# A layer with expert retrieval on one core: 32 more tokens gathered, 352 instead of 384 through all experts, gates in blocks of 16

## The chip, the core and the metric

The kernel runs on one NeuronCore of a Trainium2 chip. The core has a matrix engine (TensorE, PE in the profile; PEld is its weight load), a vector engine (VectorE, DVE), a scalar engine (ScalarE, ACT), GpSimd (POOL), which here only issues gathers, and SyncE (SP), which issues the other transfers; 16 DMA engines move the data of all queues. Each engine works through its own list of instructions in order and waits on semaphores of the others. The metric is device time in microseconds.

## What is computed

One decoder layer on 512 tokens of width 1024 in float32: a gated short convolution beside differential attention, cross-attention to 256 memory tokens, and a channel mixer that retrieves experts. The change lies in the mixer:

```python
def chunk(hc):                                    # 128 tokens
    q = (hc @ w_pq).reshape(PEER_CHUNK, PEER_HEADS, 2, PEER_DK_HALF)
    sc = jnp.einsum('thcd,chnd->thcn', q, sub_keys).astype(jnp.float32)
    vals, idx = lax.top_k(sc, PEER_TOPK)
    cand = vals[:, :, 0, :, None] + vals[:, :, 1, None, :]
    ...
    g = jax.nn.softmax(top_s, axis=-1)
    ue = peer_u[experts]
    ve = peer_v[experts]
    act = jax.nn.gelu(jnp.einsum('td,thkd->thk', hc, ue).astype(jnp.float32), approximate=False)
    return jnp.einsum('thk,thkd->td', (g * act).astype(ve.dtype), ve)
```

Each token takes 8 heads x 16 = 128 of the 16384 experts; an expert is a row of 1024 of `peer_u` and one of `peer_v`. The layer's sum is normed at the end and multiplied by `final_g`.

## The kernel before

Matrix products run in three passes of float32r: both operands are split into a high part (`hi`, ScalarE, L98) and a rest (`lo`, VectorE, L99).

The mixer treats its tokens in two ways. The first 128 tokens gather their experts' rows: for each of the 128 slots one indirect DMA brings 128 rows, one for each partition (512 KB, L825). A u row is multiplied with the token and reduced to a number on VectorE (L808); 16 of them at a time go through Gelu (L811, L812). A v row is added with its weight to an accumulator (L819). The other 384 tokens (`TY`) meet all experts: for each of 128 columns j of the 128 x 128 grid of experts an up-projection (`stage_u`: 24 matmuls of 384 columns, L120, then Gelu, L702) and a down-projection (18 matmuls of 512 columns, L757), with the activations multiplied by gates in between (L746) that are zero for experts not chosen.

The stages in order of time: selection (`keys_scores`, `keys_pairs`, on VectorE above all, with 40 up-projections beside it on TensorE), gates (`gates`), and the down loop (`experts`).

`gates` builds a 128 x 128 table for each token from one-hot rows, four tokens in a group: squares and a Relu on ScalarE (L857, L858), comparisons on VectorE (L862, L863), four matmuls (L864), a copy from PSUM (L865). Six groups make a block of `TB` = 24 tokens, which is written to DRAM (L866). Up-projections run between the groups, `BY_BLOCK` = 3 for each block.

The down loop goes over j = 0 to 127. Each j loads and splits a table of v (L740, L98, L99), reloads an activation that was spilled (L717; 64 of the 128 were spilled, L705), multiplies, splits, and does 18 matmuls. The 32 up-projections of the last columns run from j = 85 to 116, 11 ahead of their use; four more end before the loop. The gates come back for eight j at a time (L738).

The gathers are a generator, `gathered`, to which the stages `send` a number of rows: 4 for each pair of heads (`X_HEAD`), `X_BLOCK` = 3 for each block of gates, and the rest spread over the j, with weight `XW` = 3 where up-projections run beside. That is 16, 48 and 192 of 256 rows; in the loop one row for each j up to 84 and three for each from 85 to 116. A `send` copies the indices of its rows into a small tile `now` (L805; tag `e`, five buffers shared with the loop's products), works off the rows of the `send` before, and issues its own gathers. A v row's weight is copied into `now` of the `send` that works it off (L815):

```python
w = fl[:, k : k + 1]
nc.vector.tensor_copy(w, wx[:, 1, s - P : s - P + 1])
```

The order of each engine's list is made by a scheduler from this program, so instructions may stand earlier or later than they are written. At the end each block of 128 tokens gets its residual added (L771), is squared and summed (L772), goes through a root in 12 small steps, and is scaled and written (L778, L779).

## Time and profile before

| | |
|---|---|
| three runs | 2082.74, 2091.25, 2091.6 us; median 2091.25 |
| the profiled execution | 2089.85 us, of which the span of its instructions is 2088.1 |
| mean granted TensorE clock | 0.992 |
| busy | PE 96%, PEld 85%, DVE 72%, ACT 48%, POOL 17% |
| selection, with up-projections | about 880 to 1020 us |
| gates | about 1020 to 1352 us |
| down loop, one row for each j | about 1368 to 1738 us; u rows to about 1640, then v rows |
| down loop with up-projections, three rows for each j | about 1738 to 2014 us |
| rest of the loop, and the end | 2014 to 2088 us |

Times in the views are microseconds from the span's start. A matmul's duration overlaps with the next one's, so its price is taken from how many follow each other in a stretch. The idle time ahead of an instruction and what ended it stand in brackets in a timeline.

### The profile page before, as it was taken

The numbers are of one execution on the slowest core, as the hardware profiler recorded it, in microseconds if no ns is written. First come the engines' busy times: TensorE is split into PE (matmuls) and PEld (weight loads), VectorE is DVE, ScalarE is ACT, GpSimd is POOL, SyncE is SP. The second block draws the span as 40 slices with busy tenths as digits, with TensorE's granted clock in tenths as the row PEclk, the third lists the DMA queues.
The fourth block names the chain that finished last, engine by engine and source line by source line (L and its number), as shares of the span: only waits on it lengthen the run. The fifth ranks groups of instructions, "written<-read, shape, count | busy, mean of one in ns | idle before, by whom it ended". The sixth has DMA issues, their size and how long they took to land.

```text
span 2088.1 us, 29190 instructions
## 1 busy us (share of the span) xinstructions
PE 2012.8 (96%) x10341; PEld 1765.4 (85%) x10341; DVE 1503.5 (72%) x3531; ACT 1010.7 (48%) x1732; POOL 354.0 (17%) x309
## 2 busy tenths in 40 slices
PE   8999999999999999999999999999999998998997
PEld 7888888888888788999999889988877777888985
DVE  6666666423455689998787676567887776987897
ACT  6654555322344443433499999933333332332333
POOL 1000000000000000013221110022222333664440
PEclk9999999999999999999999999999999999999998
DMA  8422222334332142356778776599999888999984
GB/s 310 137 86 78 89 86 71 93 99 141 117 97 73 61 136 84 113 200 223 241 264 291 252 269 233 202 341 339 335 350 332 309 270 293 334 339 341 358 289 151
DMA packets 162418, 440.11 MB, mean 211 GB/s; under 512 B 14808, under 2 KB 70120, under 8 KB 160224
## 3 DMA queue, kind: packets, MB, share of 16 engines
q1 hardware_dynamic: 124464, 300.98, 42.9%
q0 software_dynamic: 37808, 137.26, 18.3%
q8 instruction: 81, 1.33, 0.3%
q14 instruction: 65, 0.53, 0.1%
HBM read 394.13 MB, written 46.68 MB: 211 GB/s over the span
## 4 chain that ended last, share of the span: by engine, by line
PE 47%; DMA 15%; DVE 14%; ACT 12%; issue 9%; POOL 3%; SPq 0%; ACTq 0%; DVEq 0%; POOLq 0%
PE psmm L120 33%; DMA raw<-in_peer_v 5%; ACT slot L865 5%; DMA res<-in_peer_v,e 4%; DVE lo L99 3%; PE pslg L120 3%; PE psmm L757 3%; ACT sq L857 3%; ACT hi L98 2%; PE pstr L757 2%; DMA res<-in_peer_u,e 1%; DMA act<-sp 1%; ACT oh L858 1%; DMA oh<-in_peer_v,e 1%; DVE acc L819 1%
## 5 line engine op out<-in xcount | busy, mean ns | idle before, releaser
L98 ACT ACTIVATE hi<-raw 128x1024 fp32r<-128x1024 f32 x388 | 409.8, 1059 | 605.0 <-PE psmm L120 302.1
L99 DVE TENSOR_TENSOR lo<-raw,hi 128x1024 fp32r<-128x1024 f32 x388 | 473.4, 1221 | 264.5 <-ACT hi L98 258.9
L120 PE MATMUL psmm<-A,hi 128*128 128x512 f32 x1408 | 445.9, 393 | 1.9 <-DVE Yb L457 1.9
L120 PE MATMUL psmm<-n,hi 128*128 128x384 f32 x1472 | 394.2, 345 | 1.9 <-ACT sp L702 1.9
L120 PEld LDWEIGHTS psmm<-A,hi 128*128 128x128 f32 x1408 | 262.7, 188 | 54.7 <-DVE Yb L457 2.1
L120 PE MATMUL psmm<-A,lo 128*128 128x512 f32 x704 | 277.9, 395 | 0.0
L120 PEld LDWEIGHTS psmm<-n,hi 128*128 128x128 f32 x1472 | 269.3, 190 | 2.4 <-ACT sp L702 2.3
L120 PE MATMUL psmm<-n,lo 128*128 128x384 f32 x736 | 253.0, 344 | 5.0 <-DVE lo L99 4.8
L825 POOL DMA_INDIRECT res<-in_peer_u,e x85 | 94.7, 1114 | 450.5 <-DVE e L805 422.6
L120 PEld LDWEIGHTS psmm<-A,lo 128*128 128x128 f32 x704 | 132.4, 188 | 25.2
L98 ACT ACTIVATE tr<-e 128x384 fp32r<-128x384 f32 x128 | 66.5, 520 | 179.2 <-DVE e L746 173.7
L757 PE MATMUL psmm<-hi,tr 128*128 128x512 f32 x384 | 128.4, 400 | 21.6 <-ACT hi L98 12.4
L120 PE MATMUL pslg<-n,hi 128*128 128x384 f32 x576 | 148.3, 338 | 0.0
L120 PEld LDWEIGHTS psmm<-n,lo 128*128 128x128 f32 x736 | 139.5, 190 | 7.9 <-DVE lo L99 7.8
L808 DVE CUSTOM_DVE_ANT_0 res<-res,hx 128x1024 f32<-128x1024 f32 x101 | 122.6, 1220 | 23.3 <-DMA res<-in_peer_u,e 15.8
L757 PE MATMUL psmm<-lo,tr 128*128 128x512 f32 x384 | 130.2, 393 | 0.0
L825 POOL DMA_INDIRECT res<-in_peer_v,e x74 | 106.4, 1438 | 117.6 <-DVE e L815 93.0
L825 POOL DMA_INDIRECT res<-in_peer_u,kp x16 | 20.4, 1278 | 611.3 <-DVE kp L805 548.2
L757 PE MATMUL psmm<-hi,e 128*128 128x512 f32 x384 | 119.3, 396 | 1.6 <-DVE e L805 1.6
L120 PEld LDWEIGHTS pslg<-n,hi 128*128 128x128 f32 x576 | 105.3, 188 | 3.1
L863 DVE TENSOR_SCALAR oh<-iota,e 128x128 f32<-128x128 f32 x384 | 107.1, 347 | 0.0
L757 PEld LDWEIGHTS psmm<-hi,tr 128*128 128x128 f32 x384 | 71.3, 190 | 40.0 <-ACT hi L98 13.9
(301 smaller groups left out, 3759.4 us busy)
## 6 DMA issues: line engine op xcount, KB each, us to landing
raw<-in_uT SPq DMA_DIRECT2D x128, 512.0 KB, 4.4
raw<-in_peer_v SPq DMA_DIRECT2D x128, 512.0 KB, 5.3
raw<-in_w_in SPq DMA_DIRECT2D x64, 512.0 KB, 3.5
gates<-slot SPq DMA_DIRECT2D x16, 1536.0 KB, 6.8
slot<-gates SPq DMA_DIRECT2D x16, 1536.0 KB, 11.9
act<-sp SPq DMA_DIRECT2D x64, 192.0 KB, 3.8
raw<-in_w_pq SPq DMA_DIRECT2D x16, 512.0 KB, 3.5
raw<-in_w_ckv SPq DMA_DIRECT2D x12, 512.0 KB, 7.7
```

Source lines behind the costliest of these rows:

```text
L98: self.nc.scalar.activation(hi, src, AF.Copy)
L99: self.nc.vector.tensor_tensor(out=lo, in0=src, in1=hi.bitcast(F32), op=ALU.subtract)
L120: self.nc.tensor.matmul(out, ww[:, k, :], xx, start=(k == 0 and p == 0), stop=(k == KC - 1 and p == 2))
L757: nc.tensor.matmul(accs[2 * i + half], l[:, ts], m[:, half * 512 : half * 512 + 512], start=(jj == 0 and p == 0), stop=(jj == NK - 1 and p ...
L808: nc.vector.tensor_tensor_reduce(out=t, in0=t, in1=hx, op0=ALU.mult, op1=ALU.add, scale=1.0, scalar=0.0, accum_out=wx[:, 0, s : s + 1])
L819: nc.vector.scalar_tensor_tensor(out=acc, in0=t, scalar=w, in1=acc, op0=ALU.mult, op1=ALU.add)
L825: nc.gpsimd.indirect_dma_start(out=t, out_offset=None, in_=a["peer_u"] if s < P else a["peer_v"], in_offset=bass.IndirectOffsetOnAxis(ap=i ...
L857: nc.scalar.activation(sq[:, w, :], self.iota, AF.Square, bias=it[:, t0 + w : t0 + w + 1], scale=-1.0)
L858: nc.scalar.activation(oh[:, 0:NA, :], sq, AF.Relu, bias=1.0, scale=-1.0)
L863: nc.vector.tensor_scalar(out=oh[:, 4 + w, :], in0=self.iota, scalar1=cols[:, 0, t - b * TB : t - b * TB + 1], scalar2=cols[:, 1, t - b * ...
L865: nc.scalar.copy(stage[:, :, q * 4 : q * 4 + 4].rearrange("p j w -> p w j"), pp.rearrange("p (w j) -> p w j", w=4))
```

## The change

160 tokens gather instead of 128, and 352 meet all experts instead of 384 (`MORE` = 32). The 32 additional tokens are a second set: their 128 slots lie in quarters on the partitions (partition 32 q + t holds slots 32 q to 32 q + 31 of token t), so one gather brings four rows for each of 32 tokens, and 32 gathers of u and 32 of v do them; a matmul with `quads` (four 32 x 32 identities above each other) adds the quarters at the end. Rows are now a list of jobs: 128 u, 128 v, 32 u, 32 v, 320 in all. `X_BLOCK` is 5 and there are 22 blocks of 16 tokens, so 16 + 110 rows come before the loop and 194 in it. Where there were four row buffers there are five from the gates stage on (`rx`), seven in the loop as before. Up-projections have 352 columns; `BY_BLOCK` is 2.2, and 22 blocks take 48 of them as 16 blocks of three did. The down-projection keeps 18 matmuls of 512 columns, a third of them for 96 tokens. The gates lie in DRAM in blocks of 16, so that the pieces read back are 8 x 16 instead of 8 x 24 numbers. At the end there are five parts instead of four.

```diff
-TY = NY * P
+MORE = 32
+TY = NY * P - MORE
-BY_BLOCK = 3
+BY_BLOCK = 2.2
-X_BLOCK = 3
+X_BLOCK = 5
-TB = 24
+TB = 16
...
+    def second_set(self):
+
+        nc = self.nc
+        xi, xj, xg = (e[0:MORE, 0].rearrange("p h k -> p (h k)") for e in self.e)
+        self.ex1, self.xg1 = self.t("ex1", [P, 32], I32), self.t("xg1", [P, 32])
+        for q in range(4):
+            ps, qs = slice(32 * q, 32 * q + 32), slice(32 * q, 32 * q + 32)
+            nc.vector.scalar_tensor_tensor(out=self.ex1[ps], in0=xi[:, qs], scalar=float(NK), in1=xj[:, qs], op0=ALU.mult, op1=ALU.add)
+            nc.vector.tensor_copy(self.xg1[ps], xg[:, qs])
...
-        left = 2 * P - self.rows_done
+        left = self.rows_all - self.rows_done
...
-                    ts = slice(i * P, (i + 1) * P)
+                    ts = slice(max(i * P - MORE, 0), (i + 1) * P - MORE)
+                    n = ts.stop - ts.start
...
+        quads = self.t("oh", [P, P])
+        nc.sync.dma_start(out=quads, in_=a["quads"])
+        more = [self.ps("lg") for _ in range(2)]
+        for half in range(2):
+            nc.tensor.matmul(more[half][:MORE], quads[:, :MORE], self.acc1[:, half * 512 : half * 512 + 512], start=True, stop=True)
+
+        parts = [(0, slice(0, P), [self.accx[:, :512], self.accx[:, 512:]]), (1, slice(0, MORE), more), (1, slice(MORE, P), accs[0:2])]
+        parts += [(i, slice(0, P), accs[2 * i - 2 : 2 * i]) for i in range(2, NT)]
...
+        jobs = [(0, k, v) for v in (False, True) for k in range(P)] + [(1, k, v) for v in (False, True) for k in range(32)]
+        self.rows_all = len(jobs)
...
+            if sets[1] is None and upto > 2 * P:
+                self.acc1 = self.t("acc1", [P, D])
+
+                hx1 = self.t("hx", [P, D])
+                for q in range(4):
+                    nc.sync.dma_start(out=hx1[32 * q : 32 * q + 32], in_=self.hx1)
+                sets[1] = (32, self.ex1, hx1, self.xg1, self.t("wx1", [P, 2, 32]), self.acc1)
...
-        self.turn = "e"
+        self.turn, self.tags = "e", ("rx",)
...
-        self.tags = ("oh", "oh", "row")
+        self.tags = ("oh", "oh")
```

How the lists change is shown at three places; line numbers are those of each kernel. First VectorE in the gates stage, a stretch of one block before: `oh` are one-hot rows, `res` gathered rows that are reduced against `hx`, `lo` the split of an up-projection's weights.

```order
L862 TENSOR_SCALAR oh_9706<-iota,tr_9349 128x128
L863 TENSOR_SCALAR oh_9706<-iota,e_9701 128x128 x4
L99 TENSOR_TENSOR lo_9882<-raw_9879,hi_9881 128x1024
L808 ISA res_7708,wx_7709<-res_7708,hx_6529 128x1024
L808 ISA wx_7709 128x1
L850 COPY e_10361<-tr_9355 128x24
L850 COPY e_10361<-tr_9361 128x24
L862 TENSOR_SCALAR oh_9723<-iota,tr_9349 128x128
L863 TENSOR_SCALAR oh_9723<-iota,e_9701 128x128 x4
```

And after, of the same stage:

```order
L910 TENSOR_SCALAR oh_9646<-iota,tr_9369 128x128
L911 TENSOR_SCALAR oh_9646<-iota,e_9624 128x128 x4
L856 ISA res_7719,wx_7720<-res_7719,hx_6529 128x1024
L856 ISA wx_7720 128x1
L856 ISA rx_9455,wx_7720<-rx_9455,hx_6529 128x1024
L856 ISA wx_7720 128x1
L100 TENSOR_TENSOR lo_9856<-raw_9853,hi_9855 128x1024
L851 COPY e_10112<-ex_7721 128x5
L856 ISA res_7719,wx_7720<-res_7719,hx_6529 128x1024
L856 ISA wx_7720 128x1
L910 TENSOR_SCALAR oh_9663<-iota,tr_9369 128x128
```

More than one reduction now stands between two groups of one-hot rows, and a gather takes five index columns at once; the last reduction of the stage stands ahead of its last six groups.

Second, VectorE in the down loop, a j of the first 85; before, with u rows (`slot` holds gates, `ex` the indices):

```order
L746 TENSOR_TENSOR e_13468<-B_8070,slot_13460 128x384
L99 TENSOR_TENSOR lo_13465<-raw_13462,hi_13464 128x1024
L808 ISA res_7708,wx_7709<-res_7708,hx_6529 128x1024
L808 ISA wx_7709 128x1
L99 TENSOR_TENSOR e_13471<-e_13468,tr_13470 128x384
L805 COPY e_13492<-ex_7710 128x1
```

After, three j later in the loop:

```order
L851 COPY e_13627<-ex_7721 128x1
L863 COPY e_13627<-wx_7720 128x1
L764 TENSOR_TENSOR e_13638<-B_8247,slot_13525 128x352
L100 TENSOR_TENSOR lo_13635<-raw_13632,hi_13634 128x1024
L867 SCALAR_TENSOR_TENSOR acc_13307<-res_7719,e_13627,acc_13307 128x1024
L100 TENSOR_TENSOR e_13641<-e_13638,tr_13640 128x352
L851 COPY e_13662<-ex_7721 128x1
L863 COPY e_13662<-wx_7720 128x1
L764 TENSOR_TENSOR e_13673<-B_8280,slot_13525 128x352
L867 SCALAR_TENSOR_TENSOR acc_13307<-rx_9455,e_13662,acc_13307 128x1024
```

The reduction of a u row has become the addition of a v row, which takes its weight from the index tile of the j in which it stands; the row itself was gathered with the index tile before. In the list of before the same pattern begins with the v rows, at about j = 64.

Third, TensorE at the end of the program; before:

```order
L757 MATMUL pspv_13176<-lo_18969,tr_18974 128x512
L757 MATMUL pstr_13175<-hi_18968,e_18975 128x512
L757 MATMUL pspv_13176<-hi_18968,e_18975 128x512
L940 UNCONDITIONAL_BRANCH
```

And after:

```order
L776 MATMUL pspv_13233<-lo_19068,tr_19073 128x512
L776 MATMUL pstr_13232<-hi_19067,e_19074 128x512
L776 MATMUL pspv_13233<-hi_19067,e_19074 128x512
L789 MATMUL pslg_19118<-acc_3195_17473,oh_19116 32x512
L789 MATMUL pslg_19119<-acc_3195_17473,oh_19116 32x512
L989 UNCONDITIONAL_BRANCH
```

The two matmuls with `quads` stand behind the last accumulation; on VectorE the additions of their results stand behind those of the last block, and the small steps of four parts follow in turns.

## Rows read from the trace of the kernel before

**Rows 1.** The page, busy time by engine and the DMA share in 40 slices
```profile
PE 2012.8 (96%) x10341; PEld 1765.4 (85%) x10341; DVE 1503.5 (72%) x3531; ACT 1010.7 (48%) x1732; POOL 354.0 (17%) x309
...
DMA  8422222334332142356778776599999888999984
```

**Rows 2.** Busy time by stage: stretch, its length, busy us (instructions), clock, DMA
```profile
core 0: us, PE busy (x) PEld busy (x) DVE busy (x) ACT busy (x) POOL busy (x), PEclk, DMA share, GB/s
880.00:1020.00 140.00, 134.05 (x740) 131.42 (x739) 125.90 (x342) 48.58 (x68) 25.23 (x19) 0.99 0.62 202
1020.00:1352.00 332.00, 316.92 (x2000) 306.62 (x1999) 236.69 (x671) 315.14 (x588) 48.96 (x45) 0.99 0.72 254
...
1400.00:1640.00 240.00, 235.34 (x1023) 191.27 (x1021) 190.64 (x338) 86.15 (x115) 61.59 (x56) 1.00 0.96 338
1640.00:1738.00 98.00, 91.93 (x392) 72.70 (x391) 74.54 (x131) 33.20 (x45) 33.52 (x22) 1.00 0.84 286
1700.00:1738.00 38.00, 34.43 (x147) 26.92 (x146) 28.20 (x49) 12.54 (x17) 12.56 (x9) 1.00 0.81 270
1738.00:2014.00 276.00, 263.18 (x1292) 235.76 (x1292) 228.12 (x353) 91.52 (x126) 148.57 (x98) 0.98 0.91 330
...
2075.00:2088.00 13.00, 0.00 (x0) 0.00 (x0) 9.54 (x49) 3.23 (x12) 0.00 (x0) 0.58 0.35 132
```

**Rows 3.** Chain that ended last: start, us, what; matmuls of 256, 512, 384 columns
```profile
55.65 3.77 PE psmm L120 x32
...
399.60 219.48 PE psmm L120 x961
...
1978.31 4.24 PE pslg L120 x24
```

**Rows 4.** Timelines of VectorE and of ScalarE in the gates stage: start, us, engine, line, operation
```profile
1040.08 1.22 DVE L808 CUSTOM_DVE_ANT_0 res<-res,hx 128x1024 f32<-128x1024 f32 x1
...
1041.39 0.28 DVE L862 TENSOR_SCALAR oh<-iota,tr 128x128 f32<-128x128 f32 x1
1041.59 1.11 DVE L863 TENSOR_SCALAR oh<-iota,e 128x128 f32<-128x128 f32 x4
1042.61 1.22 DVE L808 CUSTOM_DVE_ANT_0 res<-res,hx 128x1024 f32<-128x1024 f32 x1
...
1041.08 1.42 ACT L865 COPY slot<-pstr 128x512 f32<-128x512 f32 x1
1042.21 0.61 ACT L858 ACTIVATE oh<-sq 128x384 f32<-128x384 f32 x1
1042.71 0.98 ACT L857 ACTIVATE sq<-iota,tr 128x128 f32<-128x128 f32 x3
1043.58 1.05 ACT L98 ACTIVATE hi<-raw 128x1024 fp32r<-128x1024 f32 x1
```

**Rows 5.** DMA of 1020 to 1352 us, then of 1372 to 1500, there in 40 slices too
```profile
DMA packets 23353, 84.32 MB, mean 254 GB/s; under 512 B 2592, under 2 KB 9120, under 8 KB 21404
...
GB/s 403 409 393 399 252 384 300 298 294 353 350 393 401 390 288 277 234 341 322 251 306 373 366 403 404 373 307 367 374 302 264 336 365 397 405 345 265 315 285 355
DMA packets 19921, 43.64 MB, mean 341 GB/s; under 512 B 1575, under 2 KB 12071, under 8 KB 19912
```

**Rows 6.** VectorE's waits, 1400 to 1640 us, then 1640 to 1738: total, times, longest
```profile
DVE res L808 <- DMA res<-in_peer_u,e: 5.5, 5, 1.7
...
DVE acc L819 <- DMA res<-in_peer_v,e: 5.4, 3, 2.5
```

**Rows 7.** VectorE's timeline, 2030 to 2068 us: first and last multiplication of eight
```profile
2031.11 0.55 DVE L746 TENSOR_TENSOR e<-A,slot 128x384 f32<-128x384 f32 x1
...
2065.25 0.56 DVE L746 TENSOR_TENSOR e<-A,slot 128x384 f32<-128x384 f32 x1 [1.30 <-DMA res<-in_peer_v,e]
```

**Rows 8.** Timeline of the end: the last accumulation, the last scaling of two halves
```profile
2074.37 0.40 PE L757 MATMUL pspv<-hi,e 128*128 128x512 f32 x1
...
2083.40 1.42 DVE L778 SCALAR_TENSOR_TENSOR hi<-B,misc,hx 128x512 f32<-128x512 f32 x2
```

More of the change, by code (lines that the diff above doesn't have):

```diff
@@ L152, in inverse_root @@
         st = self.t("rt", [P, 8])
+        st = st[: out.shape[0]]
         v, w = st[:, 0:n], st[:, 4 : 4 + n]
@@ L673, in by_token @@
         self.x3 = self.dram.tile([NT, P, D], F32, name="x3")
-        self.hx = self.t("hx", [P, D])
+        self.hx, self.hx1 = self.t("hx", [P, D]), self.dram.tile([MORE, D], F32, name="hx1")
         for i in range(NT):
@@ L795, in gathered @@
             upto = done + more
-            if len(rows) == 4 and "row" in self.tags:
-                rows += [self.t(tag, [P, D]) for tag in self.tags]
-            assert more <= len(rows)
+            rows += [self.t(tag, [P, D]) for tag in self.tags]
+            self.tags = ()
+            if done <= P < upto:
+                self.accx = self.t("acc", [P, D])
+                sets[0] = (*sets[0][:5], self.accx)
+            if sets[1] is None and upto > 2 * P:
[4 more added lines that the diff above has]
+                sets[1] = (32, self.ex1, hx1, self.xg1, self.t("wx1", [P, 2, 32]), self.acc1)
@@ L800, in gathered @@
+            assert more <= min(len(rows), 8)
             now = self.t(self.turn, [P, 16], I32)
             fl = now[:, 8:16].bitcast(F32)
-            for s in range(done, upto):
-                if s == done or s == P:
-                    m = min(upto, P if s < P else upto) - s
-                    nc.vector.tensor_copy(now[:, s - done : s - done + m], ex[:, s % P : s % P + m])
-            for k, (s, t) in enumerate(pend):
-                if s < P:
-                    nc.vector.tensor_tensor_reduce(out=t, in0=t, in1=hx, op0=ALU.mult, op1=ALU.add, scale=1.0, scalar=0.0, accum_out=wx[:, 0, s : s + 1])
-                    if s % 16 == 15:
-                        sl = slice(s - 15, s + 1)
+            k = done
@@ new lines, in gathered @@
+            while k < upto:
+                z, c, v = jobs[k]
+                m = 1
+                while k + m < upto and jobs[k + m][0] == z and jobs[k + m][2] == v:
+                    m += 1
+                nc.vector.tensor_copy(now[:, k - done : k - done + m], sets[z][1][:, c : c + m])
+                k += m
+            for k, ((z, c, v), t) in enumerate(pend):
+                n, _, hx, g, wx, acc = sets[z]
+                if not v:
+                    nc.vector.tensor_tensor_reduce(out=t, in0=t, in1=hx, op0=ALU.mult, op1=ALU.add, scale=1.0, scalar=0.0, accum_out=wx[:, 0, c : c + 1])
+                    if c % 16 == 15:
+                        sl = slice(c - 15, c + 1)
@@ L817, in gathered @@
+                    if c == 0:
                         nc.vector.tensor_scalar(out=acc, in0=t, scalar1=w, scalar2=None, op0=ALU.mult)
@@ L927, in layout @@
     z["buckets"] = _buckets()
+    z["quads"] = np.ascontiguousarray(np.tile(np.eye(32, dtype=f), (4, 4)))
     return z
```

57 lines of the change are left out of this document (32 added, 25 removed), and 2 rows, old and new, of the table TAGS.

## The prediction

> **What bounds the kernel now.** I read the page's busy shares and its slices first, then the busy table by stage, then the chain of waits for the price of a matmul, then the waits and the order of VectorE inside the two stages that the change touches. TensorE is busy 96% of the span [rows 1], but that says little, because its matmuls are pipelined; what counts is how many end per microsecond. The chain gives the price of one behind another: 0.228 us for 512 columns, 0.177 for 384, 0.118 for 256 [rows 3]. So 384 to 352 columns saves 32 x (0.1767 - 0.1178) / 128 = 0.0147 us, 0.162 each.
>
> Four stretches matter [rows 2]. From 880 to 1020 us (selection of the pairs) VectorE is busy 125.9 of 140 us while TensorE runs up-projections beside it: both are near full. From 1020 to 1352 (gates) ScalarE is busy 315.1 of 332: it is the bound there, with VectorE at 236.7 and DMA at 0.72. From 1400 to 1738 (down-projection, one gathered row for each j) the period is set by TensorE and DMA together while u rows arrive: 1023 matmuls at 18 for a j in 240 us are 4.22 us a j against 18 x 0.228 = 4.11, with DMA at 0.96. As soon as v rows arrive the same loop takes 392 matmuls in 98 us, 4.50 us a j, with DMA down to 0.84: nothing is full, something waits. From 1738 to 2014 (down- and up-projection, three v rows for each j) it is 276 / 32 = 8.6 us a j against 18 x 0.228 + 24 x 0.177 = 8.35.
>
> **The wait in the v rows.** VectorE runs in order. A u row is only reduced, and the reduction stands some two j later in the order; a v row must be added with a weight that lies in the small index tile of the next j, so the addition stands right behind the next index copy (both orders are shown ahead). If the row hasn't landed, all of VectorE stands, and with it the split of the next gated activations that TensorE needs. The waits show it: additions wait 5.4 us for rows in res alone in the 98 us of v rows, reductions 5.5 us in the 240 us of u rows [rows 6]. In the last stretch, where DMA is at 0.6 or so, VectorE's own beat from multiplication to multiplication is (2065.25 - 2031.11) / 7 = 4.88 us, eight rows being seen [rows 7]; from 1700 to 1738, where most additions stand one index copy behind their gather, 147 matmuls in 38 us are 4.65 us a j [rows 2].
>
> **The change, part by part.** The sum is made against the profiled execution, 2089.85 us (span 2088.1), 1.4 us below the median of the three runs, 2091.25.
>
> (1) Up to the gates. TensorE saves 24 x 0.0147 = 0.353 us for each up-projection, 14.1 us for the 40 that run here. VectorE gives only part of it back: it is idle 14.1 us of 140 [rows 2], and the change adds to it two multiplications of 512 columns, 0.61 each as half of one of 1024, and eight small ones at 0.28: 3.5 us [rows 4]. VectorE's chain of selections is then what ends last; I take -1, between -6 (half of its idle time goes) and +3.
>
> (2) Gates. A group of four tokens costs ScalarE 2.50 us (copy, Relu, three squares: 1041.08 to 1043.58) and VectorE 1.22 us (1041.39 to 1042.61) [rows 4]. Eight groups of 96 go: -20 us of ScalarE, -10 of VectorE. 62 more u rows are gathered and reduced here (126 instead of 64 before the down loop): at 1.15 us each, 1040.08 to 1041.23, that is +71 us of VectorE. Three or four up-projections run earlier, -5 on each. So ScalarE comes to about 290, VectorE to 236.7 + 71 - 10 - 5 + 2 = 295. DMA: a gather is 128 rows of 4 KB, 0.524 MB; 84.3 + 62 x 0.524 - 2.1 (gates) - 0.9 (spilled activations) - 2.7 (fewer weights) = 111 MB. The highest rate that a long stretch holds is 338 to 341 GB/s [rows 2, 5], so 111 MB want 326 to 329 us: DMA becomes the bound of this stage, at almost the length that ScalarE gives it now. The last blocks' gathers are ordered ahead of the last groups, so DMA runs below its rate at the end; I add 8: 336 against 332, +4. Bounds: VectorE's 295 at the 0.95 that ScalarE reaches now, 310, is -22; 348 (DMA at 319) is +16. The hidden gain of 20 us of ScalarE is thus spent. Sixteen-token blocks make more and shorter writes, of the same rate by the packets; no cost. The gates come back in 512-byte pieces instead of 768, 22 x 128 packets for 16 x 128; at most 37% on a transfer of some 4.6 us of DMA each 8 j, 0.2 us a j, and inside the next term's bounds.
> The Trainium skill ("DMA: Bandwidth & Descriptors", section Where 436 GB/s comes from) puts the limit between HBM and SBUF at about 358 GB/s. By that the 111 MB would want 310 us, and the sum would be 2121 - 18 = 2103, inside the forecast's own range; the longest full stretch here holds 341, so the rows don't reach the page's figure.
>
> (3) Down loop, the 85 j with one row. As many rows as before, but 84 of them are v rows of the first 128 tokens, where 62 of the 85 were u rows. Now: 62 x 4.22 + 23 x 4.50 = 365 us. After: in the new order every addition stands one index copy behind its gather, so I take a beat between the 4.65 of that pattern and the 4.88 of VectorE alone, nearer the first, since about half of the additions have a weight split between: 4.70 x 85 = 399.5, +34. Bounds: 4.22 (the wait is hidden) gives -6; 5.0, 4.88 and the reloads of activations that share DMA, as they don't in either stretch, +60. The load of the second set's h, four 128 KB transfers on SP's queue, waits for the last u reduction; behind it in that queue stand the weights of j 4, which need a split behind the same reduction anyway: no cost.
>
> (4) The 32 j with up-projections: 32 x 0.353 = 11.3 us if TensorE alone decides, and 4 x 0.353 for the four at the start. DMA is at 0.91 and 330 GB/s [rows 2]; at 341 the stretch would be 267, -9. I take -9 in all, between -11 and 0.
>
> (5) Tail. Four chains of small steps instead of three end together, since the 32 tokens' sums are ready last: two multiplications by quads behind the last accumulation and about 17 more VectorE instructions behind it, at 9.54 / 49 = 0.19 us [rows 2], partly pipelined: +3, between +1 and +6. The last accumulation starts at 2074.37 and the last scaling at 2083.40 [rows 8]; all of that is on the path.
>
> Sum: -1 + 4 + 34 - 9 + 3 = +31; 2089.85 + 31 = **2121 us**.
>
> **Rivals.**
> A. The v rows hide as the u rows do: term 3 is -6, and the whole is 2089.85 - 1 + 4 - 6 - 9 + 3 = 2081. For it: the waits by name [rows 6] explain only part of 0.28 us a j, and some of it may be the change from u to v. Against it: the beat of 4.88 with DMA little loaded [rows 7].
> B. The gates stage goes at VectorE's pace and A holds too: 2081 - 26 = 2055, **faster**. It decides from the point where DMA moves over 365 GB/s for 300 us; single slices do, no long stretch does. If the gates stage does so and term 3 stands, 2095, no change. The skill's figure named above lies between this and my bound.
> C. Worse: the beat of the v rows is 5.0, since the reloads lengthen the landing, and the gates stage takes 348: 2121 + 12 + 26 = 2159.
> D. The change doesn't do what it says: a matmul of 352 columns costs what one of 384 does, because the weight load beside it decides. Term 4 goes, term 1 is +3: 2121 + 13 = 2134. Against it: 256 columns run at 0.118 with the same loads [rows 3].
>
> **How the numbers follow.** Forecast, with D in its range (2100 to 2145): 0.52. A: 0.17. B: 0.10, and its half with term 3 standing 0.05. C: 0.16. A run of this kernel tells 0.5% (10.5 us) from no change; below 2080.8 is faster, above 2101.7 slower. A splits evenly over that lower line, so faster 0.10 + 0.08 = 0.18; same 0.09 + 0.05 + 0.02 of the forecast's lower end = 0.16; slower 0.66. The range 2074 to 2160 leaves out B and the far end of C, about 0.18.
>
> **What would show it.** Matmuls of 352 columns 0.162 us apart (D if 0.177). In the gates stage DMA at 0.95 or more and ScalarE idle by over 30 us (B if ScalarE or VectorE is full). In the first 85 j a period of 4.6 to 4.9 us, DMA at 0.8 to 0.9, and VectorE's additions waiting for gathered rows; A if it is 4.2 with DMA at 0.96. After the last accumulation 16 us instead of 13.3. The forecast is wrong if that loop doesn't slow down.

## The result

The changed kernel takes 2169.9 us, median of four runs (2163.5 to 2173.1), against 2089.9 of the kernel before (median of four): a ratio of 1.039, 95% interval 1.036 to 1.042. The profiled execution took 2172.17 us, with a span of 2170.4. So it is slower by 80 us where 31 were forecast, outside the range.

The page of the changed kernel, rows as in [rows 1]: busy time by engine, then granted clock and DMA share in 40 slices of 54 us.

```profile
PE 2005.9 (92%) x10281; PEld 1726.4 (80%) x10281; DVE 1564.8 (72%) x3667; ACT 958.4 (44%) x1698; POOL 434.3 (20%) x373
...
PEclk9999999999999999998887999999999999999998
DMA  8422222343321343567998877798899978999974
```

TensorE lost four points of busy share. The gates stage lies in slices 19 to 26: the clock is lower in slices 19 to 22, and DMA stands at 0.9 in slices 20 and 21 and at 0.7 to 0.8 behind them, up to slice 26. The first matmul or the first transposition of each stage, read from both timelines, splits the 82.3 us of span:

| stretch | before | after | difference | forecast |
|---|---|---|---|---|
| start to the first transposition of the gates stage | 1020.3 | 1019.7 | -0.6 | -1 |
| to the first down-projection matmul | 348.2 | 404.4 | **+56.2** | **+4** |
| to the first up-projection inside the down loop (85 j) | 369.8 | 397.5 | +27.7 | +34 |
| to the last accumulation | 336.1 | 331.4 | -4.7 | -9 |
| tail | 13.7 | 17.4 | +3.7 | +3 |

Four of five terms are near; the gates stage is not. Its row, and those of the two parts of the down loop, answer to [rows 2]: stretch, its length, busy us (instructions), granted clock, DMA share, GB/s.

```profile
core 0: us, PE busy (x) PEld busy (x) DVE busy (x) ACT busy (x) POOL busy (x), PEclk, DMA share, GB/s
1020.00:1404.00 384.00, 308.02 (x1857) 296.50 (x1856) 299.06 (x778) 263.21 (x544) 134.45 (x105) 0.89 0.82 290
1424.00:1820.00 396.00, 370.40 (x1572) 279.88 (x1573) 287.58 (x506) 127.05 (x173) 104.83 (x84) 0.99 0.87 296
1822.00:2153.00 331.00, 310.65 (x1541) 267.00 (x1540) 269.44 (x441) 110.70 (x158) 145.75 (x107) 0.97 0.87 311
```

Over the whole gates stage nothing is full any more: ScalarE 263 of 384 us (it was 315 of 332), VectorE 299, DMA 0.82 of its time at 290 GB/s, TensorE's granted clock 0.89 where it had been 0.99. A stage that is longer than the busy time of each of its engines is a chain of waits. ScalarE's longest waits of that stretch, then VectorE's (what waited, on whom: us in total, times, longest):

```profile
ACT hi L99 <- PE psmm L121: 50.1, 21, 4.8
ACT slot L913 <- PE psmm L912: 21.4, 10, 5.9
...
ACT sp L720 <- DMA act<-sp: 13.1, 8, 4.7
...
DVE res L856 <- DMA res<-in_peer_u,e: 35.8, 21, 6.2
```

The last two have their like in the kernel before, 1020 to 1352 us:

```profile
ACT sp L702 <- DMA act<-sp: 8.6, 8, 2.7
...
DVE res L808 <- DMA res<-in_peer_u,e: 6.7, 5, 2.2
```

Two kinds of transfers are waited for: gathered rows (VectorE), and the spill of an up-projection's result to HBM (ScalarE, which can't write sp again before the last spill has landed). One block shows both, in timelines of POOL, SyncE's queue, ScalarE, VectorE and TensorE around 1200 to 1215 us (start, duration, engine and line; in brackets the idle time before it and what ended it):

```profile
1199.93 1.67 POOL L873 DMA_INDIRECT res<-in_peer_u,e  x1 [11.97 <-DVE e L851]
...
1205.64 0.94 POOL L873 DMA_INDIRECT rx<-in_peer_u,e  x1 [0.30 <-issue]
...
1200.74 5.26 SPq L723 DMA_DIRECT2D act<-sp  x2
...
1208.56 1.06 ACT L99 ACTIVATE hi<-raw 128x1024 fp32r<-128x1024 f32 x1
1214.30 0.47 ACT L720 ACTIVATE sp<-psmm 128x352 f32<-128x352 f32 x1 [4.68 <-DMA act<-sp]
1214.66 1.05 ACT L99 ACTIVATE hi<-raw 128x1024 fp32r<-128x1024 f32 x1
...
1206.39 1.23 DVE L856 CUSTOM_DVE_ANT_0 res<-res,hx 128x1024 f32<-128x1024 f32 x1 [4.09 <-DMA res<-in_peer_u,e]
...
1214.82 1.16 PE L912 MATMUL psmm<-oh 128*128 128x128 f32 x8 [1.48 <-ACT sp L720]
```

POOL was idle for 12 us until VectorE's index copy, then five gathers went out within seven. VectorE stood 4.09 us for the first of their rows. The spill issued among them (the second of the two from 1200.74, at about 1205.7) let ScalarE go on only at 1214.30, some 8.5 us later; before, the median spill of this stage landed in 3.8 us. Behind that ScalarE instruction, in its order, stood the next split of weights (1214.66) and the copies of finished gates, and TensorE waited for the PSUM bank that the spill's copy had not yet emptied.

The stage was not like this from its start. Two parts of the building, 1036 to 1126 us and 1126 to 1350, as rows and by POOL's longest wait:

```profile
1036.00:1126.00 90.00, 73.52 (x449) 71.60 (x448) 81.44 (x216) 67.24 (x142) 41.36 (x33) 0.89 0.93 339
1126.00:1350.00 224.00, 175.00 (x1028) 166.86 (x1027) 170.69 (x442) 145.19 (x298) 81.69 (x64) 0.89 0.82 285
```

```profile
POOL res L873 <- DVE wx L856: 38.0, 18, 6.3
...
POOL res L873 <- DVE e L851: 118.0, 11, 14.1
```

In the first part a gather goes out whenever a reduction (L856) frees its buffer, and DMA moves 339 GB/s at 0.93, as was forecast for the stage. In the second POOL waits for the index copy (L851), sends five gathers at once, and DMA falls to 285 GB/s at the same granted clock, 0.89. The program's order on VectorE changes in between: up to the eleventh block an index copy stands some ten rows ahead of the reductions, from the fourteenth (1199 us) on six.

The down loop shows the predicted wait, as in [rows 6] (VectorE's waits, 1424 to 1820 us): 71.9 us for v rows in 396 us, where the 98 us of v rows before showed 8.1 (5.4 in res, 2.7 in oh).

```profile
DVE acc L867 <- DMA res<-in_peer_v,e: 33.4, 17, 3.6
DVE acc L867 <- DMA rx<-in_peer_v,e: 20.1, 9, 3.9
DVE acc L867 <- DMA oh<-in_peer_v,e: 18.4, 12, 3.7
```

Two small forecasts, against [rows 3] and [rows 8]. Matmuls of 352 columns start 0.161 us apart (44 follow each other from 1205.02 to 1212.12; of them three from 1209.22 to 1209.70, the second row holding two), and from the last accumulation, 2153.00, to the last scaling it is 12.4 us instead of 9.0.

```profile
1209.22 0.32 PE L121 MATMUL psmm<-n,lo 128*128 128x352 f32 x1
1209.38 0.48 PE L121 MATMUL psmm<-n,hi 128*128 128x352 f32 x2
1209.70 0.32 PE L121 MATMUL psmm<-n,lo 128*128 128x352 f32 x1
...
2153.00 0.40 PE L776 MATMUL pspv<-hi,e 128*128 128x512 f32 x1
...
2165.41 1.40 DVE L808 SCALAR_TENSOR_TENSOR lo<-B,misc,hx 128x512 f32<-128x512 f32 x2
```

### The profile page after: what moved, and what is told of

Same layout as the page of the kernel before. It is cut to its first block, busy times and chain, and to the rows that moved or that the text cites. A ratio compares the mean times of both kernels' runs of the same rounds, so it can differ in the third digit from the quotient of the medians.

```text
span 2170.4 us, 29266 instructions
## 1 busy us (share of the span) xinstructions
PE 2005.9 (92%) x10281; PEld 1726.4 (80%) x10281; DVE 1564.8 (72%) x3667; ACT 958.4 (44%) x1698; POOL 434.3 (20%) x373
## 4 chain that ended last, share of the span: by engine, by line
PE 51%; DMA 18%; DVE 16%; issue 8%; ACT 3%; POOL 2%; SPq 1%; DVEq 0%; ACTq 0%; POOLq 0%
PE psmm L121 35%; DMA res<-in_peer_v,e 5%; DVE lo L100 4%; PE pslg L121 4%; PE psmm L776 3%; DMA oh<-in_peer_v,e 3%; DMA rx<-in_peer_v,e 2%; DMA res<-in_peer_u,e 2%; PE pstr L776 2%; DMA raw<-in_peer_v 2%; DVE acc L867 2%; POOL res L873 1%; DVE res L856 1%; DMA raw<-in_uT 1%; DVE e L100 1%
## 5 line engine op out<-in xcount | busy, mean ns | idle before, releaser
L121 PE MATMUL psmm<-n,hi 128*128 128x352 f32 x1472 | 378.4, 339 | 31.1 <-ACT slot L913 18.1
L121 PE MATMUL psmm<-n,lo 128*128 128x352 f32 x736 | 247.4, 337 | 4.2 <-DVE lo L100 4.1
L99 ACT ACTIVATE tr<-e 128x352 fp32r<-128x352 f32 x128 | 63.8, 498 | 310.9 <-DVE e L764 300.3
L873 POOL DMA_INDIRECT res<-in_peer_u,e x107 | 140.3, 1311 | 300.4 <-DVE e L851 227.8
L856 DVE CUSTOM_DVE_ANT_0 res<-res,hx 128x1024 f32<-128x1024 f32 x123 | 148.8, 1221 | 46.6 <-DMA res<-in_peer_u,e 39.2
L776 PE MATMUL psmm<-hi,tr 128*96 128x512 f32 (+1 forms) x384 | 128.8, 401 | 22.4 <-ACT hi L99 15.9
L121 PE MATMUL pslg<-n,hi 128*128 128x352 f32 x576 | 141.7, 328 | 4.1 <-ACT hi L99 4.1
L867 DVE SCALAR_TENSOR_TENSOR acc<-res,e,acc 128x1024 f32<-128x1024 f32 x91 | 116.6, 1281 | 39.9 <-DMA res<-in_peer_v,e 39.7
L776 PE MATMUL psmm<-lo,tr 128*96 128x512 f32 (+1 forms) x384 | 132.1, 398 | 7.5 <-DVE lo L100 7.5
L776 PE MATMUL psmm<-hi,e 128*96 128x512 f32 (+1 forms) x384 | 128.6, 399 | 10.9 <-DVE e L851 6.5
L776 PEld LDWEIGHTS psmm<-hi,tr 128*96 128x96 f32 (+1 forms) x384 | 64.9, 172 | 46.7 <-ACT hi L99 17.8
```

What stands on the lines that cost most here:

```text
L99: self.nc.scalar.activation(hi, src, AF.Copy)
L121: self.nc.tensor.matmul(out, ww[:, k, :], xx, start=(k == 0 and p == 0), stop=(k == KC - 1 and p == 2))
L776: nc.tensor.matmul(accs[2 * i + half][:n], l[:, ts], m[:, half * 512 : half * 512 + 512], start=(jj == 0 and p == 0), stop=(jj == NK - 1 a ...
L856: nc.vector.tensor_tensor_reduce(out=t, in0=t, in1=hx, op0=ALU.mult, op1=ALU.add, scale=1.0, scalar=0.0, accum_out=wx[:, 0, c : c + 1])
L867: nc.vector.scalar_tensor_tensor(out=acc, in0=t, scalar=w, in1=acc, op0=ALU.mult, op1=ALU.add)
L873: nc.gpsimd.indirect_dma_start(out=t, out_offset=None, in_=a["peer_v"] if v else a["peer_u"], in_offset=bass.IndirectOffsetOnAxis(ap=now[: ...
```

## The experiments

Each run is judged by three lengths from its own trace beside its median: the building of the gates (first to last ScalarE copy into the gates tile), the first 85 j of the down loop (first down-projection matmul to the first up-projection inside the loop) and the rest to the end of the span.

| run | gates built | 85 j | rest | median | ratio to before, 95% interval |
|---|---|---|---|---|---|
| before | 310.9 | 369.8 | 349.8 | 2089.9 | |
| after | 366.6 | 397.5 | 348.8 | 2169.9 | 1.036 to 1.042 |
| e1 no wait for rows | 356.9 | 399.1 | 338.6 | 2142.9 | 1.022 to 1.030 |
| e2 three rows a block | 313.9 | 390.4 | 376.6 | 2138.3 | 1.018 to 1.029 |
| e3 before, blocks of 16 | 374.8 | 386.0 | 346.3 | 2176.5 | 1.039 to 1.047 |
| e4 rows added a j later | 368.2 | 373.2 | 358.7 | 2161.7 | 1.030 to 1.040 |
| e5 e3 without row waits | 288.5 | 393.0 | 345.1 | 2134.8 | 1.019 to 1.025 |
| e6 no reductions | 358.3 | 394.9 | 346.0 | 2152.3 | 1.028 to 1.034 |
| e7 e3, rows every second block | 294.0 | 388.2 | 348.9 | 2104.0 | 1.004 to 1.010 |
| e8 before, added a j later | 312.2 | 371.8 | 342.8 | 2084.8 | 0.995 to 0.999 |
| e9 two spill buffers | 309.8 | 371.8 | 342.3 | 2083.2 | 0.995 to 0.999 |
| e10 rows spread | 350.4 | 401.3 | 342.4 | 2149.9 | 1.025 to 1.032 |
| e11 reload in one run | 371.5 | 402.4 | 335.5 | 2180.1 | 1.042 to 1.049 |
| e12 e8 and reload in one run | 312.5 | 369.2 | 331.9 | 2074.0 | 0.991 to 0.996 |
| e13 e10 and two spill buffers | 316.0 | 366.6 | 349.3 | 2082.1 | 0.995 to 1.000 |
| e14 e9, the edit of e8, and e11 together | 309.6 | 369.8 | 342.4 | 2082.7 | 0.996 to 1.000 |

The first theory (W) was that VectorE's standing on gathered rows makes the gates stage long; its rivals were the rate of the transfers (R) and the shorter blocks (S).

**e1, no wait for rows.**

```diff
-  tensor_tensor_reduce(out=t, in0=t, in1=hx, ...)
+  tensor_tensor_reduce(out=acc1_tile, in0=hx, in1=hx, ...)   # gates stage only
```

> The changed kernel, but the reductions of the gates stage read the h tile and write a spare buffer, so VectorE does the same work and stands on no gathered row there; all gathers and all their bytes stay. Left out: the products of the 110 u rows gathered in that stage are not those of the reference. Theory W (VectorE, in order, stands on rows that were gathered one block earlier into five buffers, and one-hots, TensorE and ScalarE stand behind it): the gates stage (1020 us to the first down-projection matmul, 404 us) falls to 335 to 350, the whole from 2172 to 2105 to 2120. Rival R (this mix of gathers, spills, gate writes and weights can move no more than the 290 GB/s that it showed, so the waits only show the rate): the stage stays at 395 to 404, the whole at 2160 or more. Rival S (22 blocks of 16 instead of 16 of 24 cost it, by block boundaries): also 395 or more.

The building of the gates took 356.9 us instead of 366.6. From the first transposition to the first down-projection matmul it is 405.4 us against 404.4, so the stage as a whole got no shorter: it began 20 us earlier, and that and 10 us in the last part of the loop are what the whole gained. Counted from 1020 us, as in the expectation, the stage is 386, in none of its ranges. VectorE's waits for rows, 35.8 us by name, held 10 us of the building at most, and W falls as the main cause in the changed kernel. Since nothing reads the rows here, a buffer is also free for the next gather as soon as its row has landed.

**e2, three rows a block.** X_BLOCK = 3.

> The changed kernel with three gathered rows for each block of gates instead of five: 66 rows in the stage instead of 110, 44 more in the down loop. W: the gates stage falls from 404 to 300 to 320 (ScalarE's 263 busy us less nothing, VectorE's 299 less 50), the first 85 j of the down loop grow by 5 to 15 us and the last 32 by 10 to 25 (24 rows at 1.2 us on VectorE, partly beside other work); the whole 2110 to 2130. R: 23 MB fewer at 290 GB/s are 80 us, so the stage is 320 to 325, and the same 23 MB come back in the loop, which ran at 0.88 of DMA: the whole 2150 to 2175. S: the stage stays above 380.

313.9 us of building: 53 less, for 44 rows less. That is what 44 reductions at 1.22 us take of VectorE (54), and less than their 23 MB at 290 GB/s (80). From 1020 us the stage is 347.5: less than S has (380), more than W and R have (320, 325). The loop then took the 44 rows: 376.6 us instead of 348.8 in its last part. W and R aren't told apart.

**e3, blocks of 16 alone**, in the kernel before.

```diff
-TB = 24,  BY_BLOCK = 3,  X_BLOCK = 3
+TB = 16,  BY_BLOCK = 2,  X_BLOCK = 2
```

> The kernel before with blocks of 16 alone: 24 blocks of 16 tokens, two gathered rows and two up-projections for each (48 and 48, as before). S: the gates stage, 348 us before, gets longer, by 10 us or more, and the whole is over 2100. W or R: the stage gets shorter, since the copy into the gates tile took ScalarE 1.44 us with blocks of 24 and 1.05 with blocks of 16, over 96 groups some 37 us of an engine that was busy 315 of 332: 348 to between 310 and 335, the whole 2050 to 2075.

A surprise: with as many rows as before the building took 374.8 us instead of 310.9, the whole was as slow as the changed kernel, and ScalarE was not the bound any more. The row of that stretch and VectorE's two longest waits in it:

```profile
1039.00:1413.00 374.00, 313.29 (x1868) 305.21 (x1867) 224.81 (x658) 270.52 (x562) 50.06 (x40) 0.92 0.63 210
```

```profile
DVE res L808 <- DMA res<-in_peer_u,e: 74.3, 20, 7.3
DVE e L850 <- DMA res<-in_peer_u,e: 54.4, 19, 5.8
```

129 us of VectorE's waits, with DMA at 0.63: each block copies two indices, comes to their rows two groups later and stands. By its time the run is S's; the waits say that it is W's round trip that the short blocks cost, and the next two runs ask that.

**e5 and e7: is it the round trip of the rows?** e5 is e3 with the edit of e1; e7 is e3 with four rows at every second block.

> The kernel before with blocks of 16, as in the run of blocks of 16 alone (two rows and two up-projections a block, gates stage 419.7 us instead of 348.5), but the reductions of the gates stage read the h tile and write the idle accumulator, so VectorE does the same work and stands on no row there; all transfers stay. Left out: the products of the 48 u rows gathered in that stage are not those of the reference. Theory W (with shorter blocks each block still holds a round trip of its own gathers, and VectorE stands for it: 132 us of waits for rows in that stage): the stage falls to 300 to 330 us, the whole from 2176 to 2055 to 2095. Rival S (short blocks cost by themselves: two gates tiles that change hands oftener, more and smaller writes): it stays at 390 to 420, the whole over 2140.

> The kernel before with blocks of 16 and four rows at every second block instead of two at each: same rows, same bytes, twelve round trips instead of 24. Theory W: VectorE's waits for rows halve or better, the gates stage falls from 419.7 to 330 to 360 us, the whole from 2176 to 2085 to 2120. Rival S: over 400, the whole over 2155.

```diff
-            self.gather.send(X_BLOCK)                      # 2
+            if b % 2 == 0:  self.gather.send(X_BLOCK)      # 4
```

The rows of the building stretch, e5 and then e7, and e7's wait for rows:

```profile
1080.00:1368.00 288.00, 283.72 (x1873) 282.65 (x1872) 183.90 (x583) 269.05 (x561) 40.32 (x42) 0.99 0.83 278
```

```profile
1043.00:1337.00 294.00, 285.77 (x1874) 282.80 (x1873) 223.56 (x649) 267.44 (x562) 37.47 (x37) 0.99 0.77 266
```

```profile
DVE res L808 <- DMA res<-in_peer_u,e: 20.0, 13, 4.4
```

e7 is the clean one: the same rows and the same work on VectorE (223.6 us against 224.8), half the round trips, and the building falls by 81 us to 294, 17 less than before. So blocks of 16 do free ScalarE as hoped, and what they cost is the number of round trips. e5 agrees but is not clean: reductions that read no row were moved ahead of the selections, so the stage began 46 us later and its whole missed what was expected, and VectorE had 41 us less to do inside the stretch. Of e7's gain of 17 us only four arrive at the first down-projection matmul (1364.1 for 1368.5), and its 85 j take 18 us longer than before, as those of e3 take 16. In e3's 85 j VectorE's reductions wait 28 us for u rows where they waited 9 before, and in the program's order most of them stand one index copy behind that of their own gather where most stood two behind: so blocks of 16 lengthen that loop too, likely by the place of the reader, which no run varies there alone.

**e6, no reductions**, in the changed kernel.

```diff
-  tensor_tensor_reduce(out=t, in0=t, in1=hx, ...)
+  tensor_copy(wx[:, 0, c:c+1], hx[:, 0:1])                 # gates stage only
```

> The changed kernel with the reductions of the gates stage replaced by a copy of one column: all 110 gathers and their bytes stay, VectorE is rid of some 110 x 1.15 us of work and of every wait for a row. Left out: the products of the u rows gathered in that stage. The run without the row waits left 386 us of 404. Theory V (VectorE's own work holds the rest: 30 of 32 us while rows come, and the last 60 us have no rows): the stage falls to 310 to 335 us, where the 111 MB at 340 GB/s stand, the whole to 2075 to 2105. Rival R (the transfers hold it): 365 or more, the whole over 2120.

358.3 us, as in e1, with VectorE busy 176 us of the building instead of 286. So neither VectorE's work nor its waits hold the changed kernel's stage. By the numbers that is R's range; but one slice of 32 us, 1116 to 1148, ran at 370 GB/s, so the rate is not a ceiling of this mix, though one slice doesn't refute R for a stage. What e1 and e6 share is ScalarE's wait for the spill, which grew: over the building 12.0 us by name in the changed kernel, 20.4 in e1 and 23.1 in e6, whose two longest waits of ScalarE were:

```profile
ACT hi L99 <- PE psmm L121: 48.4, 21, 5.6
ACT sp L720 <- DMA act<-sp: 23.1, 8, 6.9
```

New theory (L): rows go out in bursts, so spills land late, and with one spill buffer ScalarE, in order, stands for each.

**e9, two spill buffers**, and **e10, rows spread over a block.**

```diff
-  "sp": ("d", 1)
+  "sp": ("d", 2)
```

> The changed kernel with two buffers for the up-projection results that are spilled to HBM (sp) instead of one, so ScalarE needn't stand until the last spill has landed (it stood 13 us by name in the gates stage of the changed kernel, 25 to 28 in the runs without row waits and without reductions). The building of the gates, first to last copy, takes 366.6 us there. Theory L (the five gathers of a block come in one burst, spills and weights land late behind it, and in-order engines stand for each): 345 to 360, the whole from 2170 to 2148 to 2163. Rival R (the transfers' rate holds it): 362 or more, the whole within 6 us of the changed kernel.

```diff
-            self.gather.send(X_BLOCK)
             for q in range(TB // 4):
+                self.gather.send(2 if q == 0 else 1)
```

> The changed kernel with the five gathers of a block sent at its four groups (two, one, one, one) instead of at once: same rows, same bytes, three more index copies a block (22 x 3 x 0.17 = 11 us of VectorE). L: smaller bursts, gate building from 366.6 to 330 to 355 us, the whole 2135 to 2160. R: 360 or more. A third way: each send waits for the rows of the last one on VectorE, four round trips a block instead of one, and the stage is longer than now, 380 or more.

e10 took the time that L expects, 16 us less, but not by L's way: ScalarE's waits for spills are longer in it than in the changed kernel (17.6 us of the building against 12.0), and what fell are VectorE's waits for rows (33.8 to 11.2) and the time at a lower clock (0.89 granted in the stage, 0.96 in the row of e10 below). e9 went far beyond: one more buffer of 1.4 KB a partition took 57 us from the building, the first 85 j fell by 26, and the whole is 2083 us, slightly under the kernel before (ratio 0.997, 0.995 to 0.999). Its building stretch, and one slice of 32 us:

```profile
1033.00:1342.00 309.00, 276.20 (x1791) 268.12 (x1790) 281.20 (x741) 251.08 (x522) 133.04 (x99) 0.96 0.94 346
```

```profile
1084.00:1116.00 32.00, 30.84 (x215) 30.42 (x214) 32.00 (x87) 29.24 (x62) 17.99 (x11) 1.00 1.01 384
```

Now DMA, at 0.94 and 346 GB/s, and VectorE, busy 281 of 309 us and all of the slice, are both near full; which of them bounds the stage isn't told. But VectorE's order changed too: from the fourteenth block on the index copies stood 15 rows ahead of the reductions instead of 6, and its wait for rows was down to 3.9 us from 35.8. Most of the gain lies where the orders differ: from the fourth index copy to the tenth, with copies ten rows ahead in both, a block takes 14.1 us in the changed kernel and 13.6 in e9, from the tenth to the last 18.4 and 15.1. Buffer or order?

**e13, the spread rows with two spill buffers.** The two edits above together.

> The rows-spread kernel (gates built in 349 us, whole 2150) with two spill buffers. In the run of two spill buffers alone the order of VectorE came out differently as well: index copies stood 15 rows ahead of the reductions instead of 6, and the last reduction of the stage stood at the last group instead of ten groups earlier. Here the order of copies and reductions stays within five rows of the rows-spread kernel's, index copies four to six rows ahead in both. If the second buffer acts by itself (ScalarE no longer stands for a spill): gate building 305 to 330 us, the whole 2100 to 2130. If it was the order that came with it: 340 to 352 us, the whole 2140 to 2155.

316.0 us against 350.4, with copies three to six rows ahead of the reductions in both. The building stretch, then waits of ScalarE and of TensorE in it, of e10 and then of e13:

```profile
1031.00:1381.00 350.00, 281.61 (x1780) 268.80 (x1780) 294.19 (x822) 254.12 (x523) 136.79 (x105) 0.96 0.88 313
```

```profile
ACT hi L99 <- PE psmm L121: 56.8, 29, 5.6
ACT sp L720 <- DMA act<-sp: 17.6, 8, 7.2
ACT slot L913 <- PE psmm L912: 10.5, 7, 3.7
...
PE psmm L121 <- ACT slot L913: 20.6, 15, 2.8
PE psmm L121 <- ACT sp L720: 12.5, 10, 3.9
PE psmm L912 <- ACT sp L720: 10.4, 8, 2.8
```

```profile
1033.00:1348.00 315.00, 278.98 (x1822) 274.97 (x1822) 286.97 (x809) 251.15 (x525) 132.43 (x104) 0.95 0.95 347
```

```profile
ACT slot L913 <- PE psmm L912: 58.8, 16, 7.0
...
ACT sp L720 <- DMA act<-sp: 1.1, 1, 1.1
...
PE psmm L912 <- DVE oh L911: 31.4, 13, 4.4
PE psmm L121 <- ACT sp L720: 2.7, 3, 1.9
```

So the buffer acts by itself, and the clock doesn't explain it (0.96 and 0.95). Of the 17.6 us of spill waits 1.1 are left, and TensorE's waits for ScalarE, 43.5 us in the three rows shown, went to 2.7. That is the ring: ScalarE stands for a spill, behind it stand the splits that feed TensorE and the copy that empties its PSUM bank, TensorE falls behind, and ScalarE waits for it in turn. ScalarE's own waits for TensorE moved more than they went: before a split 56.8 to 0.3 us, before a copy of gates 10.5 to 58.8, since TensorE now waits for VectorE's one-hot rows. In all ScalarE's idle time fell by 32 us (95.9 to 63.9), and the building by 34. The whole fell further than expected, to 2082.1, because the 85 j did too, by 35 us. Spills do land later when more rows travel; issue to landing in the median, e13 and, under it, before:

```profile
act<-sp SPq DMA_DIRECT2D x54, 176.0 KB, 5.9
```

```profile
act<-sp SPq DMA_DIRECT2D x49, 192.0 KB, 3.8
```

For e10's order, then, the buffer is shown. In the changed kernel itself it isn't told apart from the order that came with it: a kernel with one spill buffer and index copies ten rows ahead all through the stage was not run, and the first part of the changed kernel's building, 339 GB/s, says that it might do as much. Two spill buffers in the kernel before were not tried; its SBUF has no room for them.

**e4 and e8, rows added one j later**, the test of the third term, in the changed kernel and in the one before.

```diff
-            for k, ((z, c, v), t) in enumerate(pend):     # rows of the last send
+            for k, ((z, c, v), t) in enumerate(old):      # of the send before it, in the loop
```

> The changed kernel, but in the down loop each gathered row is added or reduced one j later than now, so that VectorE comes to it two gathers behind. Same instructions, same transfers. Theory of my third term (VectorE in order stands on the v row of the last j): the first 85 j, about 406 us, fall to 365 to 380, and the whole from 2172 to 2125 to 2145. Rival (in this stretch DMA at 0.88 of its time and 303 GB/s is the bound, and VectorE's wait is only where it shows): under 10 us of change, and the waits move to another row.

> The kernel before, but in the first 85 j of the down loop each row is added or reduced one j later. There 23 of the 85 rows are v rows, at 4.50 us a j where the u rows run at 4.22. If VectorE's standing on v rows makes that difference: 369.8 us of that stretch become 360 to 365, the whole 2078 to 2086. If the loop's rate is set by the transfers: no change within 3 us.

e4: the 85 j fall from 397.5 to 373.2 us, as the theory of the third term says, with DMA up from 296 to 315 GB/s:

```profile
1431.00:1804.00 373.00, 368.87 (x1578) 283.38 (x1579) 299.69 (x511) 126.73 (x173) 136.56 (x84) 0.99 0.91 315
```

The whole gained only 8, less than was expected: the gates stage ended 7 us later, and what follows the 85 j took 10 us more, likely because three or four rows are in flight there for each j and two sends now share seven buffers. e8 kept the later addition out of those 32 j. By the table's length its 85 j didn't change (371.8), as the rival had it. But the v rows' part of them did:

```profile
1640.00:1740.00 100.00, 99.02 (x429) 80.09 (x428) 82.36 (x148) 36.30 (x49) 30.37 (x25) 1.00 0.89 305
```

At 18 matmuls for a j that is 4.20 us, where the 392 in 98 us of [rows 2] are 4.50, so the wait on v rows was there in the kernel before too. VectorE's multiplication of the 85th j starts 5 us sooner (1732.2 for 1737.1) though the u rows' part took 4 us longer, for a reason that no run shows; the first up-projection, which ends the table's length, comes later against it. The whole fell by 5, as the theory had it.

The same mechanism fits the loop of e9 and e13, which no edit touched. On VectorE, in the program's order, 5 of 82 additions of the changed kernel stand behind a further index copy, 46 in e9 and 64 in e13. Four rows of each, at the same j (the weight used lies in the index tile e that is named):

```
changed kernel
L851 COPY e_13732<-ex_7721 128x1
L863 COPY e_13732<-wx_7720 128x1
L764 TENSOR_TENSOR e_13743<-B_8346,slot_13525 128x352
L867 SCALAR_TENSOR_TENSOR acc_13307<-oh_13267,e_13732,acc_13307 128x1024
e9
L100 TENSOR_TENSOR e_13711<-e_13708,tr_13710 128x352
L851 COPY e_13732<-ex_7721 128x1
L867 SCALAR_TENSOR_TENSOR acc_13307<-oh_13266,e_13697,acc_13307 128x1024
L863 COPY e_13732<-wx_7720 128x1
```

Why the scheduler placed them so in e9 is not settled; that it is worth some 24 to 31 us against the changed kernel is what e4, e9 and e13 show together.

**e11, e12 and e14: the reload of the gates.** The gates lie in HBM as the down loop reads them, 16 groups of eight j.

```diff
-  dma_start(out=gt, in_=gates[:, :, j : j + GRP, :].rearrange("b i j t -> i b j t"))
+  dma_start(out=gt, in_=gates[:, g])
...
-  out = dram.tile([TY // TB, P, NK, TB])
-  dma_start(out=out[b], in_=stage)
+  out = dram.tile([P, NK // GRP, TY // TB, GRP, TB])
+  dma_start(out=out[:, :, b], in_=stage.rearrange("p (g r) t -> p g r t", r=GRP))
```

> The changed kernel with the gates kept in HBM in the order in which the down loop reads them: the reload of eight j is one run of 11 KB a partition instead of 22 pieces of 512 B, and the write of a block is 16 pieces of 512 B a partition instead of one run of 8 KB. In the kernel before with blocks of 16 the down loop took 713 to 719 us from its first to its last matmul against 701 with blocks of 24; if the shorter pieces of the reload make that, the loop here falls from 725 (1424.1 to 2148.8) by 12 to 20 us, and the gates stage grows by 0 to 8: the whole 2152 to 2164. If the loop's length comes from the order of its work and not from the pieces: within 4 us of 725, the whole 2168 to 2178.

> The kernel before with rows added one j later, as in the run of that alone (2084.8 us), and with the gates kept in HBM in the order of the reload, in blocks of 24 as before: reloads of one run instead of 16 pieces of 768 B a partition, writes of 16 pieces of 768 B instead of one run of 12 KB. If pieces under 1 KB cost the loop what blocks of 16 showed, in part: 2070 to 2082. If not: 2083 to 2092.

> The changed kernel with two spill buffers, rows added one j later in the first 85 j, and the gates kept in HBM in the order of the reload: the three edits that gained alone or in the kernel before (2083 with two buffers). If they add up: 2060 to 2075, since additions already stand a j later in the order of the two-buffer kernel and the reload gave the kernel before some 10 us. If the down loop is held by its transfers by now (0.92 of DMA in its first part): 2078 to 2090.

In both kernels the last part of the loop gained: 348.8 to 335.5 us in the changed one, 342.8 to 331.9 in e12 against e8. In the changed kernel the building and the 85 j grew by 5 each, and the runs (2167.8 to 2184.9, the profiled one at their low end) show no gain of the whole; their median is 10 us longer, outside both ranges, and nothing tells why: inconclusive there. e12 is the fastest kernel of this study: 2074.0 us, ratio 0.993 (0.991 to 0.996), better than both. It is an edit of the kernel before, and the best of the changed ones is at 2082: on this record the 32 more gathered tokens gain nothing. e14 adds up to nothing over e9 (2082.7): with two spill buffers the changed kernel has 310 us in the building and 370 to 372 in the 85 j already, and neither moved.

## Why the prediction was wrong

**Term 1** (up to the gates, -1): -0.6. Right.

**Term 2** (gates, +4): +56.2. This is the step that failed. Its quantities were right or better: 111.26 MB moved (111 forecast), VectorE 299 us (295), ScalarE 263 (290; its copy takes 1.05 us in blocks of 16, I had carried 1.42 over). The conclusion drawn from them, that DMA then binds the stage at 338 to 341 GB/s, was not. It held for the first 90 us of the building (339 GB/s at 0.93) and not behind them (285 at 0.82). I had priced rows and spills as bytes and work only, with no wait at all. They are also round trips: a single spill buffer for which ScalarE stands until the spill has landed, and rows that VectorE comes to within their own block. While ScalarE was the bound, it came to its next spill and VectorE to its rows late enough, 8.6 and 6.7 us of waits in 332, and I passed over both. With ScalarE relieved, shorter blocks and five rows at once, the waits were on the path. That the spill's wait is enough is shown for the rows-spread order (e13, 34 us of building); in the changed kernel the second buffer and the order that came with it give the 56 us back together, and their shares stay open, as does what the lower clock costs. With a second spill buffer the term would have been near: 346 GB/s at 0.94, and 348.3 us from the first transposition to the first down-projection matmul in e9, against 352 forecast. The remark that blocks of 16 cost nothing spoke of their writes, and e7 (294.0 us) doesn't contradict that; it left out the round trips, for which such blocks alone cost 64 us of building (e3).
The Trainium skill ("DMA: Bandwidth & Descriptors", section Where 436 GB/s comes from) has about 358 GB/s as the limit between HBM and SBUF; e9's 346 over 309 us lies under it, one slice of 32 us with 384 above it, and there the measurement decides. The Trainium skill ("Trainium Kernel Development and Optimization", section Best Practices) says to double-buffer so that DMA overlaps with compute; e10 and e13 agree, 34 us of the building for the second buffer of one small tile; of the 68 us of the whole another 35 lie in the 85 j, where the order of the additions changed with it.

**Term 3** (85 j, +34): +27.7, by the mechanism named: the period is 397.5 / 85 = 4.68 us (4.70 forecast), DMA 0.87, 72 us of additions waiting, and e4 takes it away. The end of the term was nearer than its size: 399.5 us forecast and 397.5 measured, but 365 taken for the 85 j before, which took 369.8.

**Terms 4 and 5** (-9 and +3): -4.7 and +3.7, inside their bounds. The 352 columns cost 0.161 us (0.162 forecast), so rival D falls.

**The rivals.** None gave the time. A (v rows hide, 2081) and the faster gates of B lacked their conditions here; e9 comes near to A's, transfers near full in the gates stage and most rows hidden in the loop, and takes 2083. C named 348 us for the gates and was far short. Missing was a rival in which no engine is full: the forecast took the longest of the busy times for the length of the stage.

## What to carry to other kernels

When a change relieves the engine that binds a stage, look for the single buffers whose transfers the in-order engines wait for, even if those waits are only some us by name now: they were hidden by the pace of the old bound, and 17.6 us of a named wait held 34 us of a stage (e10, e13), because what feeds the next engine is queued behind it. Count round trips, not only bytes: how many times in a stage an engine copies an index, sends a gather and comes to the row, and how much work lies between. Read a long stage in parts: its mean of 0.82 hid a part that ran as forecast and the point in the order at which it stopped. And before a change is given up for its time, double the smallest buffer on such a ring.

## What was not expected of the hardware

The ScalarE copy from PSUM into the gates tile (512 columns, strided write) took 1.42 us where a block has 24 tokens and 1.05 where it has 16, and 1.06 in e3, where the block's size is all that changed: so the block's size, and with it the stride of its writes (96 bytes or 64), makes the difference. The Relu behind it took 0.61 and 0.53, though its operands are the same in both; no run shows why. The mix of gathers, weights, spills and gate writes, which ran at 290 GB/s in the changed kernel, held 346 over 309 us once ScalarE no longer stood for its spills, more than the 341 of the down loop that I had taken for the ceiling.
